# Two first halves of the SSD branch product moved ahead of the mixer's last wait, and early copies out of PSUM around the products by tokens

## The chip, the core and the metric

The kernel runs on one core of a Trainium2 chip. TensorE (PE) multiplies into PSUM banks of 128 partitions x 512 floats, VectorE (DVE), ScalarE (ACT) and GpSimd (POOL) work on SBUF and PSUM, and DMAs are issued from the queues of SyncE (SP) and GpSimd. Each engine takes its own instructions in the order in which the program emits them, and waits on semaphores where an operand isn't ready or a buffer isn't free. The metric is the device time of one execution in microseconds (us). Before the change the median of three runs is 2577.49 us (2574.72 to 2578.11).

## The reference, cut to what matters

Two layers of a decoder trunk on 512 tokens of width 1024, in float32. Only the mixer in the middle of each layer is touched by the change:

```python
h = rms_norm(x, mix_norm)
q, k, v, z, xbc, dt, g_sb, g_ssm = split(h @ w_in)      # one input projection
...
# Mamba2: convolution over time, then a state-space scan
xbc = silu(causal_depthwise_conv(xbc, conv_w, conv_b))  # 4 taps and a bias, per channel
xs, bm, cm = split(xbc)                                 # 24 heads x 64; 8 groups x 128; 8 groups x 128
y = ssd_chunked_scan(xs, dt, a, bm, cm) + d_skip * xs   # 4 chunks of 128 tokens, 8 groups of 3 heads
y = y * silu(z)
y_ssm = rms_norm_per_group(y, ssm_norm) @ w_branch_ssm  # 1536 -> 1024
y_sb = stick_breaking_attention(q, k, v) @ w_branch_sb  # 512 -> 1024
x = x + (sigmoid(g_sb) * y_sb + sigmoid(g_ssm) * y_ssm) @ w_out
```

Around it stand two SwiGLU half steps (1024 to 2816 and back), and a last norm at the end.

## The kernel before

**Products.** Activations lie transposed, 128 channels on the partitions and 512 tokens along the free axis. Every float32 operand of a product is split into a high and a low part, and one block of the contraction is three matmuls (`mm3`, L359 to L361: high x high, and the two mixed terms). A *unit* is the weights of one output block: up to eight contraction blocks of 128 x 128. SP loads it (L274) into one of three `wraw` buffers, ACT casts it to `whi` (L324), DVE subtracts for `wlo` (L326). `unit_order` lists all units in the order in which they are stored and multiplied; while one is multiplied, the next two are converted and a few more are fetched. A product writes a PSUM bank `mm`, of which there are four, taken in turn. Two other pairs of banks, `pt` and `pa`, serve transposes and the small matmuls of attention and scan.

**Order.** The products are emitted in a fixed loop. Everything else is a generator that `spawn` puts on a list; after each contraction block `tick` lets every generator whose pause is over emit one more step. So the work of ACT, DVE and POOL, and the small matmuls, is interleaved with the products by numbers in the code (`yield 3` pauses for three ticks). `flush` ticks until the list is empty, with no product in between.

**The mixer.** After q, k, v and attention, one loop goes over `group_steps()`: projections of convolved blocks (x, B and C), of the gates, and products by tokens for z. Eight generators `ssd_group` run the scan of the groups beside it.

- `conv_block` takes a block from its bank `mm`: ACT writes the last tap with the bias (L1112, `cv`), DVE adds the other three taps, each reading the bank (L1115), and then the block goes through SiLU (L1120, L1127) and, for x, is transposed to tokens. It holds a buffer `raw`, of which there are three, from its start; before the change that buffer is only written at L1120.
- The x blocks are numbered 0 to 11. Blocks 4, 7 and 10 stand right in front of the products by tokens of group pairs 1, 2 and 3.
- A product by tokens (`by_tokens`, with `z_part` behind it) has four chunks of 128 tokens, each a bank of 128 x 384. `z_part` makes SiLU of z: while attention or dt isn't done, it copies the bank to SBUF first (L1173) and goes on from there with a tanh into `raw` (L1176); otherwise ACT's tanh (L1182) and DVE's gate product (L1184) both read the bank. Only the product of pair 0 goes the first way.
- `ssd_group` ends with a norm over its y: a square on ACT (L1294), a power on POOL (L1335), the product `raw` on DVE (L1343) for two heads and `acc` on ACT (L1345) for the third; these are transposed (L939, banks `pa`) and split into high and low `yt` (L1364, L1366), which makes the blocks of `y_ssm`. Groups 6 and 7 make blocks 9, 10 and 11, group 7 the last two.

**The merge.** The output blocks of the two branches are taken in `MERGE_ORDER`: 6, 7, 0 to 5. Two attention branch products (`bsb`, four contraction blocks, gated in `gated_part`, L1386) come first, then `flush`, then for each block the SSD branch product as two units of six contraction blocks into one bank (`bssm`, m, 0 and 1), its gating and addition (L1390), and the attention product two blocks on. The gates of blocks 0 to 5 were spilled to DRAM (`gd`) and come back by `refill` on SP (L1485), the first two of them right after the flush. SP's queue is one: a weight load that waits for its buffer holds what is behind it.

Of the kernel before, what the change touches and what calls it, by code (L numbers as in the profile page):

```python
# [17 lines left out]
P = 128  # L18
SEQ = 512
# [4 lines left out]
SBH = 4  # L24
# [28 lines left out]
NPAR = G_D + HEADS  # L53
EARLY = 6
FRONT = 2
MERGE_ORDER = tuple(range(EARLY, KB)) + tuple(range(EARLY))
OUT_ORDER = tuple(i // 2 + KB // 2 * (i % 2) for i in range(KB))
TAPS = KCONV + 1
# [65 lines left out]
def unit_order(layer):  # L124

    def ffn(f):
        for s, (j0, j1) in enumerate(slices(layer, f)):
            start = j0
            if s == 0 and not pairs_from(layer, f):
                for key in leading(layer, f):  # L130
                    yield key, KB
                j0 = 4
            for j in range(j0, j1):
                if j < pairs_from(layer, f):
                    yield (layer, f, "gate", j), KB
                    yield (layer, f, "up", j), KB
                elif j % 2 == 0:
                    for part in SEVEN:
                        yield (layer, f, "pair", j, part), KB
            for m in OUT_ORDER:  # L140
                yield (layer, f, "down", s, m), j1 - start

    yield from ffn(1)
    for key in leading(layer, 0):
        yield key, KB
    for t, h in qkv_order():
        yield (layer, t, h), KB
    for kind, i in group_steps():
        if kind == "z":
            for u in range(NT):  # L150
                yield (layer, "z", i, u), 2 * 2 * GW // P + (i == 0)
        else:
            yield (layer, kind, i), KB
    for m in MERGE_ORDER[:2]:
        yield (layer, "bsb", m), SBH
    for i, m in enumerate(MERGE_ORDER):
        yield (layer, "bssm", m, 0), 6
        yield (layer, "bssm", m, 1), 6
        if i + 2 < KB:
            yield (layer, "bsb", MERGE_ORDER[i + 2]), SBH  # L160
    for m in OUT_ORDER:
        yield (layer, "out", m), KB
    yield from ffn(2)
# [12 lines left out]
class Builder:  # L176
# [3 lines left out]
    AHEAD = 4  # L180
# [923 lines left out]
    def conv_block(self, kind, i, ps):  # L1104


        nc, mp = self.nc, self.mp
        r = yield from self.take("raw")
        u = yield from self.take("cv")
        _, k0 = conv_at(kind, i)  # L1110
        tap = [self.conv[:, k0 + j:k0 + j + 1] for j in range(TAPS)]
        nc.scalar.activation(u, ps, AF.Identity, scale=tap[KCONV - 1], bias=tap[KCONV])  # L1112
        yield 2
        for j in range(1, KCONV):
            nc.vector.scalar_tensor_tensor(u[:, j:], ps[:, :SEQ - j], tap[KCONV - 1 - j], u[:, j:],  # L1115
                                           op0=ALU.mult, op1=ALU.add)
            yield 1
        yield 1
        yield from self.opened()
        nc.scalar.activation(r, u, AF.Tanh)  # L1120
        yield 1
        if self.cumb is None:
            self.load_cum(0)
        dst = u
        if kind != "x":
            dst = self.ssm[i][kind] = self.t(mp, [P, SEQ], kind + "T")
        nc.vector.scalar_tensor_tensor(dst, r, 1.0, u, op0=ALU.add, op1=ALU.mult)  # L1127
        self.give("raw")
        if kind != "x":
            self.give("cv")  # L1130
        yield 3
        if kind == "x":
            p, i = divmod(i, 3)
            yield from self.meet("pt", (10, 4 + 3 * (p == 0), 10)[i])
            pt = self.transposed(dst)
            yield 1
            for g in (2 * p, 2 * p + 1):
                a, b = max(i * P, g % 2 * GW), min((i + 1) * P, (g % 2 + 1) * GW)
                if a < b:
                    if "x" not in self.ssm[g]:  # L1140
                        while not self.room["xs"]:
                            yield 1
                        self.room["xs"] -= 1
                        self.ssm[g]["x"] = self.t(mp, [P, NT, GW], "xs", bufs=3)
                    nc.scalar.activation(self.ssm[g]["x"][:, :, a - g % 2 * GW:b - g % 2 * GW],
                                         pt[:, :, a - i * P:b - i * P], AF.Copy, scale=0.5)
                    self.ssm[g]["x", i] = True
            self.give("cv")
        elif kind == "b":
            yield from self.meet("pt", 5)  # L1150
            pt = self.transposed(dst, NT - 1)
            yield 1
            tok = self.t(mp, [P, NT - 1, P], "btok")
            nc.scalar.copy(tok, pt)
            self.ssm[i]["btok"] = tok

    def z_part(self, layer, p, c, ps):

        nc = self.nc
        if p == 0:  # L1160
            if c == 0:
                self.dtx = self.t(self.nrm, [P, HEADS, NT], "rs")
            nc.vector.tensor_tensor(self.dtx[:, :, c], ps[:, 2 * GW:], self.pars[layer][:, G_DTB:G_DTB + HEADS],
                                    op=ALU.add)
            ps = ps[:, :2 * GW]
            if c == NT - 1:
                self.spawn(self.dt_stage(layer), 1)
        while not self.room["z"]:
            yield 1
        self.room["z"] -= 1  # L1170
        z = self.t(self.mp, [P, 2 * GW], "z", bufs=NT)
        if len(self.y_sb) < SBH or not self.dt_done:
            nc.scalar.copy(z, ps)  # L1173
            yield from self.opened()
            r = yield from self.take("raw")
            nc.scalar.activation(r[:, :2 * GW], z, AF.Tanh, scale=0.5)  # L1176
            yield 1
            nc.vector.scalar_tensor_tensor(z, r[:, :2 * GW], 1.0, z, op0=ALU.add, op1=ALU.mult)
            self.give("raw")
        else:  # L1180
            self.tables(False)
            nc.scalar.activation(z, ps, AF.Tanh, scale=0.5)  # L1182
            yield 1
            nc.vector.scalar_tensor_tensor(z, z, 1.0, ps, op0=ALU.add, op1=ALU.mult)  # L1184
        for g in (2 * p, 2 * p + 1):
            self.ssm[g]["z", c] = z[:, g % 2 * GW:(g % 2 + 1) * GW]
# [214 lines left out]
    def mixer(self, layer):  # L1401
# [24 lines left out]
        with ExitStack() as mix:  # L1426
# [15 lines left out]
            def branch_sb(m):  # L1442
                self.spawn(self.gated_part(self.product(self.y_sb, layer, "bsb", m), gates[m][0]))

            with tc.tile_pool(name=f"mp{layer}", bufs=2, reuse_waits="tile") as self.mp:
# [26 lines left out]
                        self.spawn(self.conv_block(kind, i, self.project(layer, kind, i)[0]))  # L1472
                for m in MERGE_ORDER[:2]:
                    branch_sb(m)
                self.flush()
            with tc.tile_pool(name=f"mg{layer}", bufs=KB, reuse_waits="tile") as mg, \
                    tc.tile_pool(name=f"gr{layer}", bufs=2, reuse_waits="tile") as gr:
                self.merged = []

                def refill(i):  # L1480

                    m = MERGE_ORDER[i]
                    gates[m] = [self.t((gp, gr)[i // 2 % 2], [P, SEQ], t) for t in ("gs", "gm")]
                    for r, src in zip(gates[m], self.gd[2 * m:2 * m + 2]):
                        nc.sync.dma_start(r, src)  # L1485
                        self.gated[r.name] = True

                def merge(i, ps):
                    yield from self.merge(ps, *gates.pop(MERGE_ORDER[i]), mg)
                    if i + 4 < KB:  # L1490
                        refill(i + 4)

                refill(2)
                refill(3)
                for i, m in enumerate(MERGE_ORDER):
                    ps = self.t(self.pmm, [P, SEQ], "mm")
                    self.dense(ps, self.unit(layer, "bssm", m, 0), self.y_ssm, 0, 6, stop=False)
                    self.dense(ps, self.unit(layer, "bssm", m, 1), self.y_ssm, 6, 12, start=False)
                    self.spawn(merge(i, ps))
                    if i + 2 < KB:  # L1500
                        branch_sb(MERGE_ORDER[i + 2])
                gain = self.pars[layer][:, G_FFN2:G_FFN2 + KB]
                branches.close()
                self.open_x()
                self.open_t()
                for m in OUT_ORDER:
                    nc.sync.dma_start(self.x[m], xd[m])
                    ps = self.t(self.pmm, [P, SEQ], "mm")
                    self.dense(ps, self.unit(layer, "out", m), self.merged, 0, KB)
                    if m == 0:  # L1510
                        self.norm_start()
                    self.spawn(self.mix_out(ps, m, gain))
# [163 lines left out]
```

## Time and profile before

| | before |
|---|---|
| median of 3 runs | 2577.49 us (2574.72 to 2578.11) |
| the profiled execution | 2577.66 us |
| its span | 2576.0 us |
| mean granted TensorE clock | 0.995 |
| busiest engines after PE | PEld, DVE, ACT |

PEld is TensorE's loading of weights, which runs beside its matmuls. An engine's row of the page gives busy time, share of the span and number of instructions. A row of the timeline gives start, duration, engine, line, operation, output and inputs without their numbers, and in brackets the idle time before it and what ended it. A row of the windows gives a stretch, its length, and for each engine the busy time with the instructions in it; the granted clock follows, where 1.00 is full speed.

Layer 0's convolved blocks begin at 499.3 us, its products by tokens for pairs 1 to 3 at 595.8, 670.3 and 742.2, and its flush ends at 821.6; in layer 1 the same places lie some 1275 us later.

### The profile page before, as it was taken

What the parts mean: (1) busy time and instruction counts of PE and PEld (TensorE: products, weight loads), DVE (VectorE), ACT (ScalarE), POOL (GpSimd) and SP (SyncE); (2) the same over time, 40 slices, a digit from 0 to 9 for tenths busy, and PEclk for the clock granted to TensorE, in tenths of its full rate; (3) what the DMA queues carried; (4) which work ended last, traced back from release to release, by engine and by line L of the source; (5) the groups of instructions that cost most, each with busy time, mean ns of one, the idle gap of its engine ahead of it and who ended that gap; (6) DMA issues with size and microseconds to landing.
All of it is one profiled execution on the core that took longest, in us unless ns stands there. A gap on an engine that the chain in (4) does not pass through costs nothing.

```text
span 2576.0 us, 39402 instructions
## 1 busy us (share of the span) xinstructions
PE 2545.2 (99%) x15536; PEld 2301.7 (89%) x15536; DVE 1795.5 (70%) x2332; ACT 1323.5 (51%) x2181; POOL 551.5 (21%) x656
## 2 busy tenths in 40 slices
PE   9999999999999999999999999999999999999998
PEld 8899998888887889989899999988888878899997
DVE  8586886666765477768896768856666644885766
ACT  6353565665554264435563445656655533653434
POOL 0131300124433001313112222001344320122220
PEclk9999999999999999999999999999999999999999
DMA  4555673232222475656656466622333234756562
GB/s 152 168 140 159 170 203 112 78 114 100 91 91 86 140 209 148 179 152 164 180 126 179 144 174 175 194 80 82 115 99 101 93 94 159 193 140 169 151 164 83
DMA packets 112874, 357.35 MB, mean 139 GB/s; under 512 B 12784, under 2 KB 20400, under 8 KB 112688
## 3 DMA queue, kind: packets, MB, share of 16 engines
q1 hardware_dynamic: 96704, 299.13, 35.1%
q0 software_dynamic: 15120, 55.06, 11.9%
q8 instruction: 122, 2.00, 0.3%
q10 hardware_dynamic: 864, 0.64, 0.1%
q14 instruction: 64, 0.52, 0.1%
HBM read 342.10 MB, written 12.68 MB: 138 GB/s over the span
## 4 chain that ended last, share of the span: by engine, by line
PE 92%; DVE 4%; ACT 2%; issue 1%; POOL 1%; DMA 0%; DVEq 0%; SPq 0%; POOLq 0%; ACTq 0%
PE mm L359 25%; PE mm L361 25%; PE mm L360 25%; PE pa L360 4%; PE pa L359 4%; PE pa L361 4%; PE pa L1268 2%; DVE wlo L326 1%; DVE cv L1115 1%; PE pa L1271 1%; ACT whi L324 1%; PE pt L939 1%; PE pt L1250 1%; PE pt L1246 0%; PE pa L498 0%
## 5 line engine op out<-in xcount | busy, mean ns | idle before, releaser
L324 ACT CAST whi<-wraw 128x1024 fp32r<-128x1024 f32 (+3 forms) x433 | 427.8, 988 | 684.2 <-PE mm L361 436.4
L326 DVE TENSOR_TENSOR wlo<-wraw,whi 128x1024 fp32r<-128x1024 f32 (+3 forms) x433 | 532.7, 1230 | 246.7 <-ACT whi L324 246.0
L359 PE MATMUL mm<-hhi,whi 128*128 128x512 f32 (+1 forms) x1472 | 501.0, 340 | 0.3 <-DVE z L1184 0.3
L361 PE MATMUL mm<-hlo,whi 128*128 128x512 f32 (+1 forms) x1472 | 494.8, 336 | 0.0
L360 PE MATMUL mm<-hhi,wlo 128*128 128x512 f32 (+1 forms) x1472 | 494.3, 336 | 0.0
L361 PEld LDWEIGHTS mm<-hlo,whi 128*128 128x128 f32 x1472 | 276.0, 187 | 30.2
L359 PE MATMUL mm<-th,whi 128*128 128x256 f32 x1080 | 302.2, 280 | 0.8 <-DVE c L648 0.8
L360 PE MATMUL mm<-th,wlo 128*128 128x256 f32 x1080 | 301.6, 279 | 0.2 <-DVE wlo L326 0.2
L359 PEld LDWEIGHTS mm<-hhi,whi 128*128 128x128 f32 x1472 | 276.4, 188 | 28.1 <-DVE z L1184 1.0
L360 PEld LDWEIGHTS mm<-hhi,wlo 128*128 128x128 f32 x1472 | 276.6, 188 | 27.6
L361 PE MATMUL mm<-tl,whi 128*128 128x256 f32 x1080 | 301.3, 279 | 0.0
L326 DVE TENSOR_TENSOR wlo<-s,whi 128x1024 fp32r<-128x1024 f32 x180 | 257.2, 1441 | 35.3 <-ACT whi L324 31.7
L359 PE MATMUL mm<-act,whi 128*128 128x512 f32 (+1 forms) x710 | 273.9, 386 | 0.0
L360 PE MATMUL mm<-act,wlo 128*128 128x512 f32 (+1 forms) x710 | 273.7, 386 | 0.0
L361 PE MATMUL mm<-act,whi 128*128 128x512 f32 (+1 forms) x710 | 273.7, 385 | 0.0
L658 POOL TENSOR_TENSOR g<-g,rs 128x512 f32<-128x512 f32 x70 | 149.3, 2132 | 481.8 <-DVE g L637 452.2
L286 POOL DMA_DIRECT2D s<-in_wflat_dram x105 | 91.9, 900 | 726.4 <-DMA s<-in_wflat_dram 630.6
L324 ACT CAST whi<-s 128x1024 fp32r<-128x1024 f32 x180 | 188.7, 1048 | 61.4 <-PE mm L361 42.2
L359 PEld LDWEIGHTS mm<-th,whi 128*128 128x128 f32 x1080 | 202.7, 188 | 1.0 <-issue 1.0
L361 PEld LDWEIGHTS mm<-tl,whi 128*128 128x128 f32 x1080 | 202.9, 188 | 0.0
L360 PEld LDWEIGHTS mm<-th,wlo 128*128 128x128 f32 x1080 | 202.2, 187 | 0.4 <-DVE wlo L326 0.4
L721 DVE SCALAR_TENSOR_TENSOR x<-mm,x 128x512 f32<-128x512 f32 x93 | 64.2, 690 | 190.2 <-PE mm L361 190.0
(310 smaller groups left out, 5311.0 us busy)
## 6 DMA issues: line engine op xcount, KB each, us to landing
wraw<-in_wflat_dram SPq DMA_DIRECT2D x321, 512.0 KB, 3.6
s<-in_wflat_dram POOLq DMA_DIRECT2D x105, 512.0 KB, 7.5
s<-in_wflat_dram SPq DMA_DIRECT2D x95, 512.0 KB, 5.1
wraw<-in_wflat_dram SPq DMA_DIRECT2D x88, 384.0 KB, 3.1
cumb<-cum_d SPq DMA_DIRECT2D x16, 768.0 KB, 4.5
xd<-x SPq DMA_DIRECT2D x16, 256.0 KB, 5.5
wraw<-in_wflat_dram SPq DMA_DIRECT2D x16, 256.0 KB, 3.4
x<-xd SPq DMA_DIRECT2D x16, 256.0 KB, 5.2
```

Of the source, the lines that this page charges most:

```text
L286: self.nc.gpsimd.dma_start(raw, self.stored(key[:-1] + (part,)), accum_op=ALU.add)
L324: nc.scalar.copy(hi[:, :n], raw[:, :n])
L326: nc.vector.tensor_tensor(lo[:, :n], raw[:, :n], hi[:, :n].bitcast(F32), op=ALU.subtract)
L359: mm(ps, a[0], b[0], start=start, stop=False, **kw)
L360: mm(ps, a[1], b[0], start=False, stop=False, **kw)
L361: mm(ps, a[0], b[1], start=False, stop=stop, **kw)
L658: eng.tensor_tensor(out, r, self.rs[:, cols].unsqueeze(1).to_broadcast([P, 2, SEQ // 2]), op=ALU.mult)
L721: self.nc.vector.scalar_tensor_tensor(x, pd, 0.5, x, op0=ALU.mult, op1=ALU.add)
L939: self.nc.tensor.transpose(pt[:, cs], src[:, cs], self.ident)
L1115: nc.vector.scalar_tensor_tensor(u[:, j:], ps[:, :SEQ - j], tap[KCONV - 1 - j], u[:, j:], op0=ALU.mult, op1=ALU.add)
L1250: nc.tensor.matmul(pu, btok[:, c, :], xws[c].rearrange("p h d -> p (h d)"), start=True, stop=True)
L1268: nc.tensor.matmul(near[:, at:at + HD], decs[c][:, i, :], xdts[c][:, i, :], start=True, stop=True)
```

## The change

**The flush.** With `AHEAD = 2` the first units of the first two merge blocks (`bssm` 6 and 7, unit 0: blocks 0 to 5 of `y_ssm`, from groups 0 to 3) are multiplied before `flush`. Their two banks stay open until the second units are added behind it. Weights are stored and fetched in the new order.

**The convolved blocks 4, 7 and 10.** ACT copies the bank into `raw` first; the pass with the bias and the three taps read `raw`.

**Chunk 0 of each product by tokens.** It always takes the way by a copy, which only pair 0 took before.

```diff
+AHEAD = 2
...
     for m in MERGE_ORDER[:2]:
         yield (layer, "bsb", m), SBH
+    for m in MERGE_ORDER[:AHEAD]:
+        yield (layer, "bssm", m, 0), 6
     for i, m in enumerate(MERGE_ORDER):
-        yield (layer, "bssm", m, 0), 6
+        if i >= AHEAD:
+            yield (layer, "bssm", m, 0), 6
         yield (layer, "bssm", m, 1), 6
...
+        if kind == "x" and i % 3 == 1 and i > 3:
+            nc.scalar.copy(r, ps)
+            ps = r
         nc.scalar.activation(u, ps, AF.Identity, scale=tap[KCONV - 1], bias=tap[KCONV])
...
-        if len(self.y_sb) < SBH or not self.dt_done:
+        if c == 0 or len(self.y_sb) < SBH or not self.dt_done:
             nc.scalar.copy(z, ps)
...
                 for m in MERGE_ORDER[:2]:
                     branch_sb(m)
+                sums = {}
+
+                def first_half(m):
+                    sums[m] = self.t(self.pmm, [P, SEQ], "mm")
+                    self.dense(sums[m], self.unit(layer, "bssm", m, 0), self.y_ssm, 0, 6, stop=False)
+
+                for m in MERGE_ORDER[:AHEAD]:
+                    first_half(m)
                 self.flush()
...
                 for i, m in enumerate(MERGE_ORDER):
-                    ps = self.t(self.pmm, [P, SEQ], "mm")
-                    self.dense(ps, self.unit(layer, "bssm", m, 0), self.y_ssm, 0, 6, stop=False)
-                    self.dense(ps, self.unit(layer, "bssm", m, 1), self.y_ssm, 6, 12, start=False)
-                    self.spawn(merge(i, ps))
+                    if i >= AHEAD:
+                        first_half(m)
+                    self.dense(sums[m], self.unit(layer, "bssm", m, 1), self.y_ssm, 6, 12, start=False)
+                    self.spawn(merge(i, sums.pop(m)))
```

How the instructions stand. The rows below are the engines' instructions in program order: line, operation, output and inputs with the program's numbers. After the change lines lie 4 to 15 further down.

TensorE at the end of layer 0's flush, before: `mm_8058` is the second attention product, `pa` the transposes of the last group's output, `mm_8141` the first merge product.

```order
L361 MATMUL mm_8058<-olo_5357,whi_7967 128x512
L939 MATMUL pa_8108<-ident,raw_8102 128x128 x4
L939 MATMUL pa_8113<-ident,acc_7830 128x128 x4
L359 MATMUL mm_8141<-yt_5914,whi_8043 128x512
L360 MATMUL mm_8141<-yt_5914,wlo_8044 128x512
```

And of the change, the same place, in two pieces: `mm_8067` is the second attention product, `mm_8103` and `mm_8136` are the first two merge products.

```order
L365 MATMUL mm_8067<-olo_5357,whi_7976 128x512
L363 MATMUL mm_8103<-yt_5915,whi_8052 128x512
L364 MATMUL mm_8103<-yt_5915,wlo_8053 128x512
```

```order
L364 MATMUL mm_8136<-yt_6940,wlo_8074 128x512
L365 MATMUL mm_8136<-yt_6941,whi_8073 128x512
L943 MATMUL pa_8167<-ident,raw_8148 128x128 x4
L943 MATMUL pa_8172<-ident,acc_7839 128x128 x4
L363 MATMUL mm_8103<-yt_7259,whi_8109 128x512
```

Between the pieces stand the rest of the 36 matmuls of the two first halves. Behind the transposes the first product goes on with its second unit (`whi_8109`), and block 6 of `y_ssm`. Elsewhere TensorE's order is as before.

ScalarE at the same flush, before: `gm` is a gate, `t` the squares of the last group, `acc` its third head, `yt` its high parts.

```order
L1376 ACTIVATE gm_8036<-mm_7961 128x512
L324 CAST whi_8064<-wraw_7962 128x768
L1294 ACTIVATE t_1400_8096,ss_7864<-y_7863 128x192 x2
L1345 ACTIVATE acc_7830<-y_7863,gny_8099 128x64 x4
L1364 ACTIVATE yt_8118<-pa_8108,par_109 128x512
L1364 ACTIVATE yt_8121<-pa_8113,par_109 128x512
L324 CAST whi_8147<-wraw_8038 128x512
```

And of the change:

```order
L1383 ACTIVATE gm_8045<-mm_7970 128x512
L328 CAST whi_8073<-wraw_7971 128x768
L328 CAST whi_8109<-wraw_8047 128x768
L1301 ACTIVATE t_1407_8121,ss_7873<-y_7872 128x192 x2
L328 CAST whi_8142<-wraw_8068 128x512
L1352 ACTIVATE acc_7839<-y_7872,gny_8130 128x64 x4
L1371 ACTIVATE yt_8177<-pa_8167,par_109 128x512
L1371 ACTIVATE yt_8180<-pa_8172,par_109 128x512
```

One more cast stands ahead of the squares and one ahead of `acc`: the units that come two places on. DVE has the matching subtractions, one ahead of `raw` (L1343) and one behind it. On SP two more loads stand ahead of the four refills of gates.

ScalarE at block 4 of layer 0 and at the product by tokens behind it, before: `mm_5806` is the block's bank, `mm_5897` and `mm_5917` those of chunks 0 and 1.

```order
L1112 ACTIVATE cv_5908<-mm_5806,conv_4679 128x512
L1364 ACTIVATE yt_5914<-pa_5883,par_109 128x512
L324 CAST whi_5951<-wraw_5807 128x768
...
L324 CAST whi_6075<-wraw_5946 128x1024
L1182 ACTIVATE z_6095<-mm_5897 128x384
L1182 ACTIVATE z_6108<-mm_5917 128x384
```

And of the change:

```order
L1117 COPY raw_5907<-mm_5806 128x512
L1119 ACTIVATE cv_5908<-raw_5907,conv_4679 128x512
L1371 ACTIVATE yt_5915<-pa_5883,par_109 128x512
L328 CAST whi_5952<-wraw_5807 128x768
...
L328 CAST whi_6076<-wraw_5947 128x1024
L1180 COPY z_6096<-mm_5897 128x384
L1183 ACTIVATE raw_6098<-z_6096 128x384
L1189 ACTIVATE z_6111<-mm_5918 128x384
```

One copy is added in each, in the first reader's place; DVE's three taps and its gate product stand where they did, and read `raw` and `z` instead of the bank. POOL's order doesn't change. In both layers together ACT has 12 instructions more.

## The prediction

> **What bounds the kernel now.** I read the head of the page first, then the chain that ended last, then TensorE's waits by what ended them, and last the timeline and the windows around the longest of those waits.
>
> ```profile
> PE 2545.2 (99%) x15536; PEld 2301.7 (89%) x15536; DVE 1795.5 (70%) x2332; ACT 1323.5 (51%) x2181; POOL 551.5 (21%) x656
> PE 92%; DVE 4%; ACT 2%; issue 1%; POOL 1%; DMA 0%; DVEq 0%; SPq 0%; POOLq 0%; ACTq 0%
> ```
>
> TensorE is busy for 99% of the span and is 92% of the chain. No matmul is added or removed, so the change can win only where TensorE waits, or where it runs at less than its full clock. The profiled execution took 2577.66 us, 1.66 more than its span of 2576.0 and 0.17 over the median of 2577.49. The sum below starts from 2577.66.
>
> ```profile
> PE mm L359 <- DVE cv L1115: 11.1, 6, 2.7
> PE pa L939 <- DVE raw L1343: 7.5, 2, 3.7
> ...
> PE mm L359 <- DVE z L1184: 0.3, 2, 0.2
> ```
>
> The columns are the total, the count and the longest. Six waits end with a convolution tap (L1115), two with the normalised product of the last SSD group (L1343), two with a gate product (L1184). These are just the three places that the diff touches, and the rest of the table of waits is about 1 us at most in each row.
>
> ```profile
> 592.78 0.34 PE L361 MATMUL mm<-wlo,hhi 128*128 128x384 f32 x1
> 595.81 0.41 PE L359 MATMUL mm<-whi,hhi 128*128 128x384 f32 x1 [2.69 <-DVE cv L1115]
> ...
> 670.30 0.41 PE L359 MATMUL mm<-whi,hhi 128*128 128x384 f32 x1 [0.87 <-DVE cv L1115]
> ...
> 742.23 0.41 PE L359 MATMUL mm<-whi,hhi 128*128 128x384 f32 x1 [1.99 <-DVE cv L1115]
> ...
> 817.52 0.39 PE L361 MATMUL mm<-olo,whi 128*128 128x512 f32 x1
> 821.64 0.69 PE L939 MATMUL pa<-ident,raw 128*128 128x128 f32 x4 [3.73 <-DVE raw L1343]
> ...
> 1871.53 0.41 PE L359 MATMUL mm<-whi,hhi 128*128 128x384 f32 x1 [2.68 <-DVE cv L1115]
> ```
>
> The four waits of layer 0 and one of layer 1. The first three are at the start of a product by tokens (128x384): its first chunk needs the PSUM bank of a convolved block whose three taps have not all run. The fourth is the flush, where nothing is left to multiply until the last group's output can be transposed. A wait costs a little more than its label, because the pipe drains: from 592.78 to 595.81 are 3.03 us where two such matmuls stand 0.17 apart, which is 2.86 for a label of 2.69. I add 0.16 to each of the eight.
>
> ```profile
> 596.80:600.20 3.40, 3.40 (x14) 3.31 (x13) 1.56 (x2) 1.51 (x3) 0.00 (x0) 0.50 0.02 5
> 743.60:746.90 3.30, 3.30 (x15) 3.20 (x14) 1.56 (x2) 1.75 (x3) 0.00 (x0) 0.50 0.00 0
> 822.10:825.40 3.30, 3.30 (x12) 2.82 (x11) 2.10 (x3) 1.88 (x3) 0.00 (x0) 0.50 0.00 0
> 2016.80:2020.10 3.30, 3.30 (x11) 3.30 (x12) 0.11 (x1) 1.36 (x2) 0.00 (x0) 0.50 0.00 0
> 2095.30:2102.00 6.70, 5.99 (x18) 5.08 (x19) 2.67 (x4) 2.82 (x7) 0.00 (x0) 0.50 0.24 77
> 1871.60:1875.00 3.40, 3.40 (x24) 3.36 (x24) 0.93 (x2) 1.96 (x3) 0.00 (x0) 1.00 0.00 0
> ```
>
> Stretches behind those waits: length, busy time (instructions) of PE, PEld, DVE, ACT and POOL, then the granted clock. In five of them the clock is at 0.50. So most waits cost twice, once as idle time and once as a slow stretch behind it. Behind the wait at 1871.53 the clock stayed at 1.00 though the wait was as long as the one at 595.81, so this second price isn't paid every time.
>
> **The sum of what can go.** Idle: 11.1 + 7.5 + 8 x 0.16 = 19.9 us. Half clock: PE was busy for 3.40 + 3.30 + 3.30 + 3.30 + 5.99 = 19.29 us at 0.50, and half of it, 9.6, is lost. The gate product adds 0.3. Together 29.8 us, of which the flush holds 7.5 + 0.3 + (3.30 + 5.99) / 2 = 12.4 and the rest is at the products by tokens.
>
> [...]
>
> **Part 1, the convolved block (three in each layer).**
>
> ```profile
> 589.53 0.77 ACT L1112 ACTIVATE cv<-mm,conv 128x512 f32<-128x512 f32 x1
> 665.40 0.77 ACT L1112 ACTIVATE cv<-mm,conv 128x512 f32<-128x512 f32 x1
> 737.87 0.77 ACT L1112 ACTIVATE cv<-mm,conv 128x512 f32<-128x512 f32 x1
> ...
> 593.02 0.74 DVE L1115 SCALAR_TENSOR_TENSOR cv<-mm,conv,cv 128x511 f32<-128x511 f32 x1
> 593.68 0.55 DVE L1260 TENSOR_TENSOR dec<-pt,dec 128x384 f32<-128x384 f32 x1
> 594.14 1.52 DVE L1115 SCALAR_TENSOR_TENSOR cv<-mm,conv,cv 128x510 f32<-128x510 f32 x2
> ...
> L643 ACT COPY g<-mm 128x512 f32<-128x512 f32 x45 | 26.4, 588 | 71.0 <-PE mm L361 71.0
> ```
>
> ACT had read the bank by 590.30, but the taps hold it until 595.66. After the change ACT's copy stands where the first pass stood, and copies of this shape take 0.588 us: the bank is free at about 590.2, against a need at 592.95 (592.78 + 0.17). Likewise at the other two blocks: ACT's first pass starts at 665.40 and 737.87, so the banks come free about 666.1 and 738.5, needed at 669.3 and 740.1 (the starts 670.30 and 742.23 less what their waits cost). Layer 1 has the same three. The six waits go whole. The price is one ACT copy each, 6 x 0.59 = 3.5 us, behind which ACT had idled until the next cast:
>
> ```profile
> 596.96 0.83 ACT L324 CAST whi<-wraw 128x768 fp32r<-128x768 f32 x1 [6.07 <-PE mm L360]
> ```
>
> That cast waits for matmuls, so it moves with TensorE, and 6 us of idle time cover the 0.59. Uncovered it would be at most 3.5 us in all.
>
> The taps then read two SBUF operands instead of PSUM and SBUF. No tap does that in this trace; the nearest row of either kind:
>
> ```profile
> L1115 DVE SCALAR_TENSOR_TENSOR cv<-mm,conv,cv x168: 734/746/752, 499.3 to 2062.9; 128x511 f32<-128x511 f32 x56, 128x510 f32<-128x510 f32 x56, 128x509 f32<-128x509 f32 x56
> ...
> L1127 DVE SCALAR_TENSOR_TENSOR cv<-raw,cv x24: 679/692/1057, 539.0 to 2052.4; 128x512 f32<-128x512 f32 x24
> ```
>
> By its min and max (679 and 1057, against the median of 746) the 18 taps cost between 1.2 us less and 5.6 us more of DVE time. I take no change, near the median of 692. It isn't on the path, since the taps no longer hold a bank; what they feed, the transposes of this block, comes after the whole product.
>
> [...]
>
> **What is late next.** DVE and the group's chain, which do not get faster.
>
> ```profile
> 600.77 1.00 PE L1268 MATMUL pa<-xdt,dec 128*128 128x64 f32 x8
> ...
> 674.88 1.01 DVE L1260 TENSOR_TENSOR dec<-pt,dec 128x384 f32<-128x384 f32 x2
> ...
> 677.51 0.56 PE L1268 MATMUL pa<-xdt,dec 128*128 128x64 f32 x4
> ```
>
> L1260 multiplies the decay that L1268 then needs. At the first product it ends at 594.23 (593.68 + 0.55), 6.5 us ahead of the matmuls, and TensorE will come about 4.5 earlier (2.85 of wait and 1.7 of slow clock). At the second it ends at 675.89, 1.6 ahead, and TensorE comes 1.03 earlier. The third stands about like the first, with 3.8 to come. All hold, the second by half a microsecond or less, since a weight load stands ahead of the matmul. I leave 0.4 us for it; if it didn't hold, DVE would be the bound there (rival B).
>
> **Part 2, the first chunk of each product by tokens.**
>
> ```profile
> 756.23 1.05 ACT L324 CAST whi<-wraw 128x1024 fp32r<-128x1024 f32 x1 [0.75 <-PE mm L360]
> ...
> 760.09 0.55 DVE L1184 SCALAR_TENSOR_TENSOR z<-z,mm 128x384 f32<-128x384 f32 x1 [1.55 <-ACT z L1182]
> ...
> 760.70 0.50 PE L359 MATMUL mm<-hhi,whi 128*128 128x512 f32 x1 [0.17 <-DVE z L1184]
> ...
> L1173 ACT COPY z<-mm 128x384 f32<-128x384 f32 x8 | 3.9, 482 | 4.0 <-DVE rs L1163 4.0
> ```
>
> The bank is held until DVE's gate product ends at 760.64 and TensorE takes it at 760.70. ACT's tanh ends just before 760.09, and a copy of this shape (0.48) in its place frees the bank there, about 0.57 earlier. The tanh follows from SBUF at about the same price, so ACT does 6 x 0.5 = 3 us more, ahead of the next decay exponentials, on an engine that is busy for 51%. Since TensorE will come up to 3.8 us earlier here, 0.57 is enough only because ACT's work ahead of it is itself let go by TensorE (the cast at 756.23 waited for L360). I leave 0.4 us for what is not carried along.
>
> **Part 3, the flush.** Two first halves, 36 matmuls, now stand behind the second attention product.
>
> ```profile
> 825.76 0.39 PE L360 MATMUL mm<-yt,wlo 128*128 128x512 f32 x1
> ...
> 827.80 0.39 PE L360 MATMUL mm<-yt,wlo 128*128 128x512 f32 x1
> ...
> 820.80 1.06 ACT L1345 ACTIVATE acc<-y,gny 128x64 f32<-128x64 f32 x4 [1.42 <-POOL gny L1335]
> ...
> 820.80 0.69 DVE L1343 TENSOR_TENSOR raw<-y,gny 128x512 f32<-128x512 f32 x1 [2.17 <-POOL gny L1335]
> ...
> 815.89 0.33 SPq L1485 DMA_DIRECT2D gs<-gd  x1
> ```
>
> Nine matmuls stand between 825.76 and 827.80, 0.227 each; 36 take 8.2 us, from 817.75 to 825.9. The group's output was ready at 821.49 and 821.86. A subtraction and a cast of a later unit now stand ahead of these, so I put them at 822.2 and 823.9: 2 us of slack, and the wait goes whole. The 36 matmuls are missing later, where TensorE is never idle, so they cost nothing. Behind the transposes only 12 matmuls (2.7 us) now cover the last two blocks' scaling, ready about 829 for a need at 830; at most 1 us per layer hangs on it. On SP two loads of the new units go ahead of the four gate refills (at 815.89 before), and the second waits for a weight buffer: I put the refills at 820. They are needed when the third merge row is gated, near 834.
>
> Sum: 2577.66 - 29.8 + 0.4 + 0.4 = 2548.7 us. By the median before it would be 2548.5, which is no difference.
>
> **Rivals.** A: the wait of the third product by tokens comes back at the first chunk's bank. For it speaks that TensorE follows the release by 0.06 us; against, that ACT's row there is driven by TensorE. It gives back up to 3.8 us in each layer less 0.57, and with a slow stretch of 1.7 us, 6.5 to 10: 2555 to 2559.
>
> B: DVE, not the bank, holds the products by tokens; the next wait is for L1260. For it speaks the thin 1.2 us of the second product; against, that the other two have 5.6. If nothing of the conv part came through, the flush's 12.4 would remain: 2577.66 - 12.4 + 0.4 = 2565.7.
>
> C: the three stretches at 0.50 at products by tokens stay, because something other than these waits sets them. They hold (3.40 + 3.30 + 3.30) / 2 = 5.0 us: 2577.66 - 24.8 + 0.8 = 2553.7. Against it: each stands right behind a wait.
>
> D, slower: the four gate refills. If the two weight loads hold SP's queue beyond 834 instead of 820, DVE stands at the gating (L1386), the subtractions of the next weights queue behind it, and TensorE stops. It decides from a slip of 14 us on; to eat the gain of 29 in two layers it must reach a further 15 us in each, to over 849, which would give about 2580 or more. Against it: the load ahead of them needs only a buffer that a subtraction like those already there sets free.
>
> E: no change, when the group's chain simply ends as late as before in all six places and the flush's gain is lost as well, 2577.
>
> **How the numbers follow.** Forecast 0.76, A 0.12, B 0.05, C 0.02, D 0.03, E 0.02. The range goes from 2545.2 (all of the 29.8 without a remainder, 2547.9, less the 2.8 by which the lowest run lay under the median) to 2557 (within A, and the 5.6 of the taps). 0.2%, or 5.2 us, is about what a measurement of this kernel can tell from no change. Faster: the forecast, A, B and C, 0.95; same 0.02; slower 0.03.
>
> **What would show it.** The rows of waits for L1115 and L1343 are gone from TensorE's table; its granted clock has no stretch at 0.50 around the products by tokens and the flush; 36 merge matmuls stand between the attention product and the transposes, with no idle label on the transposes. If a wait for `z` or for `dec` stands at the products by tokens, A or B holds; if slow stretches remain without waits, C; if a weight subtraction behind L1386 releases TensorE in the merge, D. The forecast is wrong by most if DVE falls behind for a whole group, since I have priced its slack only at the three places.

## The result, and the profile after

The changed kernel takes 2546.41 us (median of 4 runs, 2545.87 to 2546.98), the kernel before in the same comparison 2576.10. The ratio is 0.9885, 95% interval 0.9867 to 0.9902: faster by about 30 us, or 1.2%. The profiled execution took 2546.98 us (span 2545.3) against 2577.66 before, 30.7 less; 29.0 less was forecast.

The head of the page after the change: busy time, share and count of each engine, then the chain that ended last.

```profile
PE 2534.1 (100%) x15536; PEld 2293.7 (90%) x15536; DVE 1796.7 (71%) x2332; ACT 1328.9 (52%) x2193; POOL 557.7 (22%) x656
PE 96%; DVE 2%; DMA 1%; issue 1%; ACT 1%; SPq 0%; POOL 0%; DVEq 0%; ACTq 0%; POOLq 0%
```

TensorE's count is the same, but its busy time fell by 11.1 us. Most of that, 9.6 us by the sum of the prediction, is the second price of the waits: the same matmuls, fewer of them at a clock of 0.50. DVE's and ACT's shares of the chain fell from 4% and 2% to 2% and 1%. All that is left of TensorE's table of waits:

```profile
PE pt L1566 <- DVE ones L518: 1.1, 1, 1.1
PE pa L1058 <- DVE state L457: 0.6, 2, 0.3
PE pt L773 <- ACT g L760: 0.2, 1, 0.2
PE mm L364 <- DVE wlo L330: 0.2, 1, 0.2
```

The rows for the taps (11.1), for `raw` (7.5) and for `z` (0.3) are gone, and nothing has taken their place. The row for `c` (0.8 before, in the last feed-forward step, which the change doesn't touch) is gone too. The windows over the places where TensorE had waited: stretch, length, busy time of PE, PEld, DVE, ACT and POOL with their instructions, granted clock.

```profile
591.00:599.00 8.00, 8.00 (x55) 7.96 (x55) 7.06 (x12) 4.38 (x9) 1.83 (x3) 1.00 0.21 69
...
735.00:742.00 7.00, 7.00 (x48) 6.96 (x48) 5.55 (x9) 2.51 (x7) 2.77 (x5) 1.00 0.26 85
808.00:822.00 14.00, 14.00 (x67) 11.70 (x66) 5.31 (x7) 5.12 (x13) 3.28 (x5) 1.00 0.42 138
2062.00:2076.00 14.00, 14.00 (x71) 11.92 (x70) 7.28 (x11) 5.64 (x15) 5.00 (x9) 1.00 0.40 128
```

TensorE is busy throughout, at a clock of 1.00. The same holds at the second product of layer 0, from 664 to 671 us.

How each place now runs, from the timelines of ACT, DVE and TensorE. The first convolved block in front of a product by tokens:

```profile
590.53 0.58 ACT L1117 COPY raw<-mm 128x512 f32<-128x512 f32 x1
...
590.69 0.47 PE L363 MATMUL mm<-whi,hhi 128*128 128x384 f32 x1
...
593.98 0.33 PE L363 MATMUL mm<-whi,hhi 128*128 128x384 f32 x1
...
595.15 1.53 DVE L1122 SCALAR_TENSOR_TENSOR cv<-raw,conv,cv 128x510 f32<-128x510 f32 x2
```

The product by tokens starts at 590.69. Each of its chunks takes six matmuls before the next chunk begins, and the nineteenth matmul, at 593.98, opens the fourth chunk, which is given the block's bank because the four banks are taken in turn. The bank has been free since 591.11, 2.9 us earlier. The taps end only at 596.68, as long after the product's start as before the change (6.0 us); they just hold nothing any more.

This also sets right where TensorE had waited. The times 595.8, 670.3 and 742.2 above, and the "first chunk" of the prediction, are not the starts of the products: before the change the first product began at 589.68, and 595.81 is the start of its fourth chunk. Next, chunk 0 of the third product by tokens:

```profile
751.18 0.46 ACT L1180 COPY z<-mm 128x384 f32<-128x384 f32 x1
751.95 0.39 PE L363 MATMUL mm<-hhi,whi 128*128 128x512 f32 x1
752.23 0.56 DVE L1185 SCALAR_TENSOR_TENSOR z<-raw,z 128x384 f32<-128x384 f32 x1 [2.10 <-ACT raw L1183]
```

Here only 0.31 us lie between the end of the copy and TensorE's use of the bank, in layer 1 as well; behind the other two products it is 2.0 and 4.4 us. And the flush, with SP's first refill:

```profile
808.90 0.39 PE L363 MATMUL mm<-yt,whi 128*128 128x512 f32 x1
...
811.34 0.42 SPq L1500 DMA_DIRECT2D gs<-gd  x1
...
812.12 0.69 DVE L1350 TENSOR_TENSOR raw<-y,gny 128x512 f32<-128x512 f32 x1 [1.19 <-POOL gny L1342]
...
813.75 1.06 ACT L1352 ACTIVATE acc<-y,gny 128x64 f32<-128x64 f32 x4
...
817.07 0.60 PE L943 MATMUL pa<-ident,raw 128*128 128x128 f32 x4
```

The 36 matmuls run from 808.90 to 817.07; `raw` is ready at 812.81 and `acc` at 814.81, so the transposes start without a wait.

### The profile page after: what moved, and what is told of

Same layout as the page of the kernel before. It is cut to its first block, busy times and chain, and to the rows that moved or that the text cites. A ratio compares the mean times of both kernels' runs of the same rounds, so it can differ in the third digit from the quotient of the medians.

```text
span 2545.3 us, 39422 instructions
## 1 busy us (share of the span) xinstructions
PE 2534.1 (100%) x15536; PEld 2293.7 (90%) x15536; DVE 1796.7 (71%) x2332; ACT 1328.9 (52%) x2193; POOL 557.7 (22%) x656
## 4 chain that ended last, share of the span: by engine, by line
PE 96%; DVE 2%; DMA 1%; issue 1%; ACT 1%; SPq 0%; POOL 0%; DVEq 0%; ACTq 0%; POOLq 0%
PE mm L363 26%; PE mm L364 26%; PE mm L365 26%; PE pa L364 4%; PE pa L363 4%; PE pa L365 4%; PE pa L1275 2%; PE pa L1278 1%; PE pt L1257 1%; PE pt L943 1%; PE pt L1253 1%; DVE wlo L330 1%; PE pa L943 0%; PE pa L1060 0%; DMA s<-in_wflat_dram 0%
```

## The experiments

Each was timed in five rounds against the kernel before on the same chip, apart from one that was only profiled. The 23 runs of the kernel before that stood beside them lay between 2574.3 and 2580.2 us.

**The first halves alone.** Without the copies of the blocks and of chunk 0.

```diff
-        if kind == "x" and i % 3 == 1 and i > 3:
-            nc.scalar.copy(r, ps)
-            ps = r
...
-        if c == 0 or len(self.y_sb) < SBH or not self.dt_done:
+        if len(self.y_sb) < SBH or not self.dt_done:
```

> Only the two first halves ahead of the flush; blocks 4, 7, 10 and chunk 0 as before. Theory (each wait goes where its cover stands, and with it the slow stretch behind it): the row of TensorE's waits for the normalised product raw (7.5 us) is gone, the taps' row stays at 11.1 us in 6 waits. Gain 7.8 us idle and two slow stretches (3.30 and 5.99 us busy at half clock, so 4.6): about 12 us, ratio 0.9953, time near 2564. Rival (the last group's chain was only the first of several late things): a new wait of 2 us or more at the transposes or at the second halves, and less than 7 us gained.

2564.42 us against 2576.18, ratio 0.9953 (0.9941 to 0.9966), 11.8 us less. Its table of TensorE's waits begins with

```profile
PE mm L363 <- DVE cv L1119: 11.1, 6, 2.7
```

The flush's row is gone, the taps' row is what it was to a tenth, and no new one came. Apart from the last microseconds of the program (at 0.50 also in the kernel before, from 2569.69 us on, and in the change, from 2540.82), the clock was at 0.50 behind four of the taps' waits and nowhere else; its mean was 0.996. The flush is worth what its own wait and slow stretches held.

**The copies of the blocks alone.** `AHEAD` at 0 and chunk 0 as before.

```diff
-AHEAD = 2
+AHEAD = 0
...
-        if c == 0 or len(self.y_sb) < SBH or not self.dt_done:
+        if len(self.y_sb) < SBH or not self.dt_done:
```

> Only the copy of blocks 4, 7 and 10; no first half ahead of the flush, chunk 0 as before. Theory: the taps' row of 11.1 us is gone, the flush's two waits stay (7.5 us). Gain 12.1 us idle and the slow stretches behind products by tokens (about 5): 17 us, ratio 0.9934, time near 2559. At the bank of chunk 0 of the third product the copy left 0.3 us of slack in the trace of the change; without it the bank comes free 0.57 later, so waits of 0.1 to 0.5 us in each layer. Rival A of the prediction: there the wait comes back with up to 3.2 us in each layer and a slow stretch behind it, 6 to 10 us, time near 2567.

2558.74 us, ratio 0.9931 (0.9917 to 0.9944), 17.4 us less. The waits:

```profile
PE pa L943 <- DVE raw L1350: 7.5, 2, 3.7
...
PE mm L363 <- DVE z L1191: 0.4, 2, 0.2
```

The two halves add up: 11.8 + 17.4 = 29.2, where the whole change has 29.7 in the same comparison. Here the clock was at 0.50 behind the two waits of the flush alone, apart from the program's end; its mean was 0.997. At chunk 0's bank the wait that rival A feared is 0.4 us by its labels in both layers together.

**The change without its copy of chunk 0.**

```diff
-        if c == 0 or len(self.y_sb) < SBH or not self.dt_done:
+        if len(self.y_sb) < SBH or not self.dt_done:
```

> The change without its copy of chunk 0 (first halves and block copies stay). Theory: chunk 0's bank of the third product comes free 0.57 us later with 0.3 of slack: a wait for z of 0.1 to 0.5 us in each layer, no slow stretch, time 0 to 1 us over the change (2546 to 2548). Rival A: ACT's tanh doesn't move with TensorE, waits of 2 to 3.2 us in each layer, time 2552 to 2556.

2547.38 us against 2546.47 for the change itself, 0.9 more, with ranges that overlap (2546.03 to 2548.46, and 2545.84 to 2546.76). The time alone can't tell them apart, but the timeline of TensorE can:

```profile
751.75 0.50 PE L363 MATMUL mm<-hhi,whi 128*128 128x512 f32 x1 [0.17 <-DVE z L1191]
```

The wait is the same 0.17 us as in the kernel before, though TensorE comes here about 9 us earlier. So ACT's tanh did move with TensorE, and the copy of chunk 0 is worth some 0.33 us in each layer: without it two matmuls start 0.50 us apart here (751.25 and 751.75) and not 0.17. Rival A's 6 to 10 us had no ground.

**The change itself, once more.**

> The change itself on the same chip, as the yardstick: 2546.4 (2545.9 to 2547.0). Theory (no wait long enough to cost clock is left, so nothing depends on where the clock's windows fall): its runs spread by about 1 us, against about 4 for the kernel before. Rival (the spread of the kernel before comes from elsewhere, DMA for one): both spread alike.

2546.47 us, 2545.84 to 2546.76: a spread of 0.9 us against 3.3 for the kernel before in the same comparison. This agrees with the theory, and the next run shows what makes the kernel before spread. It isn't the whole of the spread, though: `no_z_copy`, the change without its copy of chunk 0, has 2.4 us between its lowest and highest run, and `conv_most` below has 3.8, both with a granted clock of 0.999 in every run. Where that comes from, no run here shows.

**The kernel before, profiled once more.**

> The kernel before, profiled once more. [...] Rival (the place in the program decides): the same five places show 0.50 again.

One run of 2580.95 us, 3.3 us over the first profile. TensorE's waits at these places are the same:

```profile
PE mm L359 <- DVE cv L1115: 11.1, 6, 2.7
PE pa L939 <- DVE raw L1343: 7.5, 2, 3.7
```

But the slow stretches are not all the same. The five places of the first profile show 0.50 again; at layer 0's flush the stretch is now 6.70 us long where it was 3.30, and at layer 1's it is the reverse. A sixth has come, at the wait of 1873.78, which had cost no clock in the first profile (there at 1871.53). So the place in the program doesn't decide it alone. The windows of this run, and that wait:

```profile
596.50:599.90 3.40, 3.21 (x10) 3.25 (x11) 0.04 (x1) 1.24 (x2) 0.00 (x0) 0.50 0.02 5
743.30:746.60 3.30, 3.30 (x11) 3.30 (x11) 0.24 (x1) 1.36 (x2) 0.00 (x0) 0.50 0.00 0
821.80:828.50 6.70, 6.01 (x19) 5.09 (x20) 2.64 (x4) 2.79 (x7) 0.00 (x0) 0.50 0.20 69
1873.10:1879.80 6.70, 6.02 (x21) 5.95 (x22) 2.10 (x3) 1.96 (x3) 0.00 (x0) 0.50 0.06 10
2023.30:2026.60 3.30, 3.30 (x16) 3.20 (x14) 1.56 (x2) 1.62 (x3) 0.00 (x0) 0.50 0.00 0
2101.80:2105.10 3.30, 3.30 (x12) 2.73 (x11) 2.10 (x3) 1.88 (x3) 0.00 (x0) 0.50 0.02 5
...
1873.78 0.66 PE L359 MATMUL mm<-whi,hhi 128*128 128x384 f32 x1 [2.65 <-DVE cv L1115]
```

Counted in stretches of 3.41 us, the length of the shorter ones in the first profile (596.79 to 600.20 the first of them), that profile had six around these waits and this one has eight. Two more at 1.7 us each (half of 3.41 is lost at 0.50) fit the 3.3 us by which it took longer. The same waits thus cost a different amount from run to run. The kernel without them has neither this loss nor this part of the spread.

**One first half, and three.** `AHEAD` at 1 and at 3 in the changed kernel.

```diff
-AHEAD = 2
+AHEAD = 1
```

> The change with one first half ahead of the flush instead of two (18 matmuls, 4.1 us of cover instead of 8.2). Theory: the wait before was 3.73 us, so one half covers it nearly: raw is ready 4.1 us after the last attention matmul, acc at most 0.5 us later than the cover ends. Waits of 0 to 0.6 us in each layer, no slow stretch, time 0 to 1.5 us over the change. Rival (the casts and subtractions of the units ahead push acc back as they do in the change, where it is ready 6.1 us after the last attention matmul): waits of 2 us in each layer, and perhaps slow stretches, 4 to 8 us over the change.

2546.14 us (2545.77 to 2546.89), no different from the change. The flush of layer 0:

```profile
810.92 1.07 ACT L1352 ACTIVATE acc<-y,gny 128x64 f32<-128x64 f32 x4 [1.41 <-POOL gny L1342]
...
812.36 0.60 PE L943 MATMUL pa<-ident,acc 128*128 128x128 f32 x4
```

`acc` is ready at 811.99, 0.4 us ahead of its transposes: one half is just enough. In the change `acc` is later only because a cast that waits for the end of the first half stands ahead of it.

```diff
-AHEAD = 2
+AHEAD = 3
```

> The change with three first halves ahead of the flush (12.2 us of cover). Theory: cover beyond the 6.1 us that acc needs buys nothing and costs nothing: within 1 us of the change; the four gate refills, behind one more weight load, issue 2 to 5 us later after the last attention matmul than in the change (2.4 us there) and still ahead of their use. Rival D: a load that waits for its buffer holds SP's queue until after the gating needs the refills; DVE waits for the gates and TensorE for weight subtractions, 2 us or more over the change.

2546.19 us (2545.88 to 2547.13). The refills come late, but not too late; SP's queue, and what the gating of a refilled gate waits for on DVE:

```profile
814.56 0.42 SPq L1500 DMA_DIRECT2D gs<-gd  x1
...
DVE gs L1393 <- PE mm L365: 3.4, 4, 1.4
```

The last attention matmul ended its turn near 808.0, so the refills issue 6.6 us behind it, against 2.4 in the change. DVE still waits only for TensorE there, never for a refill. Rival D stays far off even with one load more in the queue.

**The copy for blocks 3 to 11.**

```diff
-        if kind == "x" and i % 3 == 1 and i > 3:
+        if kind == "x" and i > 2:
```

> The change with the copy for x blocks 3 to 11 of each layer, 18 instead of 6. Theory: banks of the other blocks were not waited for and ACT has room, so nothing: within 1 us of the change, with 12 more copies of 0.58 us on ACT. Rival (the cover of the copies is thin: ACT is late elsewhere): up to 12 x 0.62 = 7.4 us over the change, with TensorE waiting for casts or banks that ACT sets free.

2549.01 us (2548.59 to 2549.38), some 2.6 us slower than the change; run again it took 2549.29. My expectation was wrong: more copies are not free. The waits have a new row; behind it stand the rows of layer 0's block 11, in this run and then, at the same place, in the change.

```profile
PE pt L943 <- DVE cv L1134: 1.3, 2, 0.7
...
764.45 2.76 DVE L1122 SCALAR_TENSOR_TENSOR cv<-raw,conv,cv 128x511 f32<-128x511 f32 x3
...
764.68 0.97 POOL L1290 TENSOR_TENSOR y<-y,t 128x192 f32<-128x192 f32 x1 [3.19 <-DVE t L1286]
765.61 1.05 POOL L1294 TENSOR_TENSOR y<-y,z 128x192 f32<-128x192 f32 x1
766.62 0.97 POOL L1247 TENSOR_SCALAR_AFFINE_SELECT dec<-dec 128x384 f32<-128x384 f32 x1
...
768.66 0.36 ACT L1301 ACTIVATE t<-y 128x192 f32<-128x192 f32 x1 [1.51 <-POOL y L1294]
...
769.02 0.62 ACT L1127 ACTIVATE raw<-cv 128x512 f32<-128x512 f32 x1
...
770.74 0.63 PE L943 MATMUL pt<-ident,cv 128*128 128x128 f32 x4 [0.65 <-DVE cv L1134]
```

```profile
765.00 2.31 DVE L1122 SCALAR_TENSOR_TENSOR cv<-mm,conv,cv 128x511 f32<-128x511 f32 x3
...
765.22 0.60 POOL L1290 TENSOR_TENSOR y<-y,t 128x192 f32<-128x192 f32 x1 [3.19 <-DVE t L1286]
765.78 0.60 POOL L1294 TENSOR_TENSOR y<-y,z 128x192 f32<-128x192 f32 x1
766.34 0.52 POOL L1247 TENSOR_SCALAR_AFFINE_SELECT dec<-dec 128x384 f32<-128x384 f32 x1
...
768.29 0.62 ACT L1127 ACTIVATE raw<-cv 128x512 f32<-128x512 f32 x1
```

The delay comes through GpSimd. In both runs the taps start right behind the same DVE instruction, so the copy itself delays nothing, and the 0.45 us that the taps take longer isn't on the path either: they end at 767.21, 1.8 us before ACT's tanh (L1127) starts. But the three GpSimd instructions beside them take 2.99 us where they took 1.72. A second square on ACT (L1301) waits for a GpSimd product behind these three, and the tanh stands behind that square in ACT's order. So the tanh starts 4.6 us after the first tap and not 3.3, and the transposes, which have little room, wait for what follows from it. Layer 1 shows the same.

**The copy for blocks 3 to 10**, to see whether block 11 is the cause.

```diff
-        if kind == "x" and i > 2:
+        if kind == "x" and 2 < i < 11:
```

> The kernel of conv_all (2549.0 us, 2.6 over the change) without the copy of block 11, so blocks 3 to 10. Theory (in conv_all block 11's copy, slower first pass and taps put its transposes 0.65 us late, a wait that was not there before): the two waits of L943 for cv (1.3 us by their labels, 1.6 from start to start) are gone, time 1.5 to 2 us under conv_all, 2547.0 to 2547.5; what is left over the change is smaller than a measurement can tell. Rival (ACT is late in general, each further copy costs): the time falls by about a sixth of the 2.6 us, to 2548.6.

2547.43 us (2545.80 to 2549.60), and the row of L943 is gone. The GpSimd instructions beside block 11's taps, which read the bank again, are back at 0.60, 0.60 and 0.52 us. So block 11 is the place, as the theory had it, though the way is by GpSimd and not by the slower first pass and taps. By the median, 1.9 us went with it; the runs spread too widely to put a figure on what is left. The yardstick beside it:

> conv_all once more on the same chip, as the yardstick for conv_most: 2549.0 (2548.6 to 2549.4), with the two waits of L943 for cv again.

2549.29 us (2548.42 to 2550.05), with the row of L943 at 1.3 us again.

## Why the prediction was right

**The bound.** TensorE's waits, with the slow stretches behind them, were the whole of what could be won, and in the profiled executions the time fell by 30.7 us where the sum held 29.8. Of the 0.9 between them the row for `c` would be 0.8; the change doesn't touch that place, and the row comes and goes among the runs. Worked from the second profile of the kernel before, with its eight slow stretches, the same sum (20.2 us idle, 12.6 at half clock) gives 2580.95 - 32.8 + 0.8 = 2549.0 us, so the forecast doesn't hang on where the slow stretches of one run fell.

**The convolved blocks.** Forecast 17.1 us (the 17.4 at the products by tokens without chunk 0's 0.3) less 0.4 for DVE; the part alone gave 17.4. The copies took 0.574 to 0.582 us (0.588 assumed). That DVE and the group's chain would just hold was right where it was said to be thinnest: the decay product is 0.33 us ahead of TensorE's next need behind the second product by tokens. Behind the first and third it is 1.3 and 0.9, where the working left 2 and more. At the first it looked at the matmul that reads the decay, and an earlier one needs the bank that the decay is taken from; the third had 4.5 us before the change (741.43 to 745.98), not 6.5 like the first. The 0.4 set aside was not spent. The taps:

```profile
L1122 DVE SCALAR_TENSOR_TENSOR cv<-mm,conv,cv x150: 734/748/751, 500.3 to 2040.1; 128x511 f32<-128x511 f32 x50, 128x510 f32<-128x510 f32 x50, 128x509 f32<-128x509 f32 x50
L1122 DVE SCALAR_TENSOR_TENSOR cv<-raw,conv,cv x18: 739/744/1099, 594.0 to 1998.1; 128x511 f32<-128x511 f32 x6, 128x510 f32<-128x510 f32 x6, 128x509 f32<-128x509 f32 x6
```

The median is nearly unchanged, as assumed, and the maximum is 1099, a little beyond the bound of 1057. Of the 18 taps the ten with no GpSimd instruction beside them took 739 to 751 ns; of the other eight, four took as little and four took 881 to 1099. Of 85 taps that read PSUM beside GpSimd none took over 751. What the prediction left out is the other side: it priced what the taps lose, not what GpSimd loses beside them. At block 10's taps two GpSimd instructions of each layer took 957 to 971 ns, against medians of 512 and 521, and GpSimd's busy time rose from 551.5 us to 557.7. Here it cost nothing, because nothing on the path waited for them; at block 11 in the experiment ACT did.

**Chunk 0.** The forecast left 0.4 us; no wait was left. The mechanism, that ACT is carried along by TensorE, is shown by the run without this copy, where the wait kept its 0.17 us. The chance of 0.12 for rival A was too high: the rows already showed whom ACT waited for.

**The flush.** Forecast 12.4 us, 11.8 alone. 36 matmuls took 8.17 us (8.2 forecast); `acc` was ready 2.3 us before the transposes (2.0); refills issued 2.4 us behind the last attention matmul (820 against 817.75 in the prediction). What I did not see is that one half would have done: I took the ready time of `acc` behind the casts of two halves as given.

**The clock.** Forecast 9.6 us; TensorE's busy time fell by 11.1. Where the other 1.5 us come from is not shown. Rival C fell: in both single parts the slow stretches went where the waits went, and stayed where they stayed. The other rivals saw nothing: B's wait for the decay product did not come, D's refills were never waited for, E's chain let go of all six places.

## What to carry to other kernels

If the bound engine waits for a buffer that a slow reader holds, one copy by an idle engine frees it early, but look at what runs beside the readers that now read the copy. The same edit is free at six blocks here. At block 11 of each layer GpSimd's three instructions beside the taps took longer with it (2.99 us against 1.72 in layer 0), and for them ACT waited, and then TensorE for 0.7 us. To cover a wait, the stall's own length (3.7 us here, against 4.1 us of cover from one half) says how much independent work is enough; in these runs more of it bought nothing and cost nothing. A wait of 2 us on TensorE cost nearly twice its length here (1.99 us idle before 742.23, and 1.7 lost in the slow stretch behind it), and that second price varied from run to run (nothing behind the wait at 1871.53, and 6.70 us at 0.50 around the same wait in the second profile).

## What the runs showed of the hardware

In the first profile of the kernel before, the clock was at 0.50 in five stretches behind the waits that the change takes away: four of 3.41 us (596.79 to 600.20 the first of them) and one of 6.83 (2095.24 to 2102.07). The waits ahead of them were 2.0 to 3.7 us long. Behind the two shortest, 0.87 us before 670.30 and 0.86 before 1944.45, the clock was at 1.00.

The length of a wait alone didn't decide whether a slow stretch followed. Behind 2.69 us before 595.81 one did, behind 2.68 us before 1871.53 none did, and around the same wait in the second profile, 2.65 us before 1873.78, the clock was at 0.50 for 6.70 us. What decides is not shown.

Where a tap that read two SBUF inputs and GpSimd instructions overlapped, both took longer in some cases. In the change four of eight such taps took 0.88 to 1.10 us, the other four 0.74 to 0.75 like those with no GpSimd instruction beside them, and GpSimd instructions with medians of 0.51 and 0.52 us took 0.96 and 0.97 beside the four slow ones. With the copy at block 11 of layer 0 three GpSimd instructions beside the taps took 0.97, 1.05 and 0.97 us, without it 0.60, 0.60 and 0.52. With one input from PSUM the taps of the change stayed at 0.75 us or less. By what way they slow each other is not shown.
